# One hybrid mixer layer on Trainium2: high halves of split weights moved to ScalarE, SBUF-port exclusion put into the scheduler's model, two roots and their scans placed earlier, and the first step's low halves on VectorE

## The chip, the cores and the metric

The kernel runs on one core of one Trainium2 chip. The metric is the time on the device in microseconds (us), the median of three runs. The instruction engines are TensorE (PE in the profile, with its weight loads as PEld), VectorE (DVE; V in the code), ScalarE (ACT; A), GpSimd (POOL; G) and the DMA queues, which are issued from SyncE (SP).

## What is computed

A decoder trunk of two layers runs over T = 272 tokens (16 learned meta tokens ahead of 256) of D = 1024 channels. Layer 0's mixer is one projection whose columns feed two heads side by side (SSD and RG-LRU), then one output projection; layer 1's mixer is a multiscale causal pooling. Each layer ends in a hierarchical mixture of experts (MoE). Only layer 0's mixer is touched here:

```python
def ssd_lru_mixer(hn, w_in, ..., w_out):
    proj = hn @ w_in
    z, xbc, dt_raw, lru_gate, lru_in = jnp.split(proj, [i1, i2, i3, i4], axis=-1)
    y_ssd = ssd_mixer(z, xbc, dt_raw, ...)
    xb = causal_depthwise_conv(lru_in, lru_conv_w, lru_conv_b)
    y_lru = rg_lru(xb, lru_w_a, ...) * jax.nn.gelu(lru_gate, approximate=True)
    return jnp.concatenate([y_ssd, y_lru], axis=-1) @ w_out
# end of ssd_mixer: one root mean square for each of 2 groups of 512 channels
    y = y.reshape(bsz, l, SSD_WIDTH) * jax.nn.silu(z)
    yg = yg * lax.rsqrt(jnp.mean(yg * yg, axis=-1, keepdims=True) + RMS_EPS)
# in rg_lru: a root for each channel and token, then a scan along the tokens
    mult = jnp.sqrt(-jnp.expm1(2.0 * log_a))
    u = mult * (i * xf)          # h[t] = a[t] * h[t-1] + u[t]
```

## The kernel before, in words

The engines' program is recorded first and ordered afterwards. A class `Program` wraps the engines; each call is recorded as an `Op` with an estimated duration, and `order()` places the recorded ops on the engines by a list scheduler that works on those estimates. It also fills gaps of TensorE with small dummy products (`wm`, L735 at the start). So every instruction shows the recorder's line, L102, in the profile, and tiles rather than lines tell them apart. A change of an estimate, or of where a piece of work is recorded, changes the order of the instructions on every engine.

`mixer0()` runs in 26 steps of 256 weight columns. Steps 0 to 17 multiply the normed tokens by `w_in`, steps 18 to 21 multiply the SSD output `ys` by the upper half of `w_out`, steps 22 to 25 the LRU output `yl` by the lower half. The products are made in a reduced format at nearly full precision: each operand is split into a high half and a low half, and three products are added (Xh·wh, Xl·wh, Xh·wl). With 8 slices of 128 input channels (`k`), 2 blocks of 128 columns and 3 products, a step has 48 matmuls into two PSUM tiles `pj`.

The f32 weight tile `w` of a step is split in three parts by the plan `SPLIT_IN`/`SPLIT_OUT`: slices 0 to 3 (tiles of 128x1024) and 4 and 5 (128x512) get their high half `wh` from ScalarE and their low half `wl` = w − wh from VectorE; slices 6 and 7 get both halves from GpSimd. A pool of 7 buffers holds them, so that a step's halves can only be made when a buffer of about two steps earlier has been read. `split_act` makes the halves of `ys` and `yl`: ScalarE the high one, GpSimd the low one. In step 0, whose parts are split finer, slices 0 to 3 have other makers: VectorE makes some high halves, GpSimd the low ones.

Between the projections stands the heads' own work, placed by `at(step, function)`: the conv, gates and quads of the SSD (`mq`, `yp`, `xT`), the gated and normed SSD output (`z_gate`, whose sums of squares over 512 channels go through TensorE products `gss`; `group_norm` with its root on ScalarE and its reciprocal `rg` on VectorE), the LRU's gates (`lru_gates`, tiles `lr`, `li`, `xb`), its root (`lru_sqrt`, one ScalarE instruction on 8 tiles `lq`) and its 8 scans (`lru_scan`), then `lru_out` with the gate. Before, `z_gate` stands at step 15, `lru_sqrt` and `group_norm` at 16, the scans at 17 and 18.

Weight tiles are loaded by SyncE in a fixed order into 17 slots; the table `HELD` sets how many slots the heads' tiles keep at each step. After the mixer comes the MoE, whose expert weights stream through the same slots.

## Time and profile before

| | |
|---|---|
| runs | 737.16 us median of 3 (736.65 to 738.29) |
| profiled execution | 736.74 us; its span 735.1 us |
| mean granted TensorE clock | 0.978 of full speed |
| PE / DVE / ACT / POOL busy | 696.8 / 314.8 / 245.2 / 148.8 us |
| bytes moved | 234 MB, 318 GB/s over the span |

The mixer of layer 0 takes the first 215 us or so of the span. The busy times are sums over the whole span; a row of the timeline has the start in us from the span's start, the busy time in us, the engine, the line, the operation, the tiles (output, then inputs), the shapes and the number of equal instructions in a row; in square brackets stand the idle time of the engine just before it and what ended that.

### The profile page before, as it was taken

Reading aid. Unit: us, or ns where it says so; the run is one execution under the profiler, and the core shown is the slowest. Engines: PE = TensorE matmul, PEld = TensorE weight load, DVE = VectorE, ACT = ScalarE, POOL = GpSimd, SP = SyncE. Lnnn points to the kernel's source line nnn. Section 1 sums busy time; section 2 is a strip of 40 time slices with the busy share of each in tenths; the row PEclk is TensorE's granted clock in tenths of the full one; section 3 lists DMA queues with packets and bytes.
Section 4 is the critical chain, followed back from the end, with each engine's and each line's share of the span. In section 5 each row is a group of like instructions: output and inputs, shape, how many; then the busy total and the mean of one; then the engine's idle time right before and its main releaser. Section 6 shows DMA issues by size and latency. Waiting matters only on the chain. (4 is left out here: it accounts for less than half of the span.)

```text
span 735.1 us, 10978 instructions
## 1 busy us (share of the span) xinstructions
PE 696.8 (95%) x4309; PEld 442.7 (60%) x4309; DVE 314.8 (43%) x701; ACT 245.2 (33%) x466; POOL 148.8 (20%) x149
## 2 busy tenths in 40 slices
PE   6999999997999999999996999999999999989995
PEld 5989898997899556346343544585444453443344
DVE  6879799769965312022022014544120220302114
ACT  5565485785353232112110301452212121121114
POOL 5554685557751000000000012000000000000003
PEclk7999999999999999999998999999999999999998
DMA  8994021945574879999999999998799999999995
GB/s 258 242 349 151 20 63 62 326 135 214 207 284 170 290 293 411 409 409 409 409 409 408 409 399 377 400 408 306 296 405 409 408 409 409 409 408 408 409 385 155
DMA packets 99622, 234.06 MB, mean 318 GB/s; under 512 B 12700, under 2 KB 51800, under 8 KB 99560
## 3 DMA queue, kind: packets, MB, share of 16 engines
q1 hardware_dynamic: 97448, 232.72, 84.0%
q8 instruction: 37, 0.61, 0.3%
q10 hardware_dynamic: 2112, 0.52, 0.3%
q14 instruction: 25, 0.20, 0.1%
HBM read 232.18 MB, written 1.05 MB: 317 GB/s over the span
## 5 line engine op out<-in xcount | busy, mean ns | idle before, releaser
L102 PE MATMUL yb<-w,ht 128*64 128x512 f32 (+2 forms) x592 | 114.9, 538 | 2.3 <-ACT ht L102 2.0
L102 PE MATMUL gb<-w,xg 128*64 128x512 f32 x496 | 114.0, 597 | 0.0
L102 PE MATMUL ub<-w,xg 128*64 128x512 f32 (+1 forms) x514 | 112.9, 581 | 0.0
L102 PE MATMUL pj<-Xh,wh 128*128 128x272 f32 x288 | 85.8, 300 | 1.3 <-DVE xT L102 1.3
L102 PE MATMUL pj<-Xl,wh 128*128 128x272 f32 x288 | 84.4, 294 | 0.0
L102 PE MATMUL pj<-Xh,wl 128*128 128x272 f32 x288 | 84.1, 293 | 0.0
L102 PEld LDWEIGHTS ub<-w,xg 128*64 128x64 f32 x514 | 37.4, 137 | 70.5 <-issue 68.8
L102 PEld LDWEIGHTS yb<-w,ht 128*64 128x64 f32 x592 | 40.6, 137 | 64.4 <-issue 53.7
L102 DVE SCALAR_TENSOR_TENSOR yl<-yb,gs,yh 128x512 fp32r<-128x512 f32 (+2 forms) x37 | 25.1, 677 | 124.6 <-ACT yh L102 115.4
L102 DVE SCALAR_TENSOR_TENSOR sg<-ub,gs,sg 128x512 f32<-128x512 f32 x16 | 12.0, 751 | 153.4 <-PE ub L102 152.0
L102 PEld LDWEIGHTS gb<-w,xg 128*64 128x64 f32 x496 | 33.6, 136 | 61.1 <-issue 57.5
L102 DVE TENSOR_TENSOR wl<-w,wh 128x1024 fp32r<-128x1024 f32 (+1 forms) x50 | 59.5, 1200 | 16.8 <-PE pj L102 9.1
L102 ACT ACTIVATE xg<-xgp,gain_e 128x256 f32<-128x256 f32 x64 | 30.2, 475 | 97.2 <-PE xgp L102 78.7
L102 POOL TENSOR_TENSOR fo<-hT,gfin 128x256 f32<-128x256 f32 (+1 forms) x10 | 6.1, 630 | 277.7 <-DVE hT L102 277.5
L102 POOL TENSOR_SCALAR wh<-w 128x512 fp32r<-128x512 f32 x25 | 52.1, 2084 | 31.9 <-PE pj L102 23.9
L102 DVE TENSOR_TENSOR hT<-cmb,hT 128x272 f32<-128x272 f32 (+3 forms) x102 | 44.9, 495 | 29.7 <-PE cmb L102 29.6
L102 PEld LDWEIGHTS pj<-Xh,wh 128*128 128x128 f32 x288 | 55.4, 194 | 2.7 <-DVE xT L102 1.5
L102 ACT ACTIVATE yh<-yb,gs 128x512 fp32r<-128x512 f32 (+2 forms) x37 | 23.3, 630 | 98.2 <-PE yb L102 98.2
L102 PEld LDWEIGHTS pj<-Xl,wh 128*128 128x128 f32 x288 | 55.4, 193 | 0.2
L102 PEld LDWEIGHTS pj<-Xh,wl 128*128 128x128 f32 x288 | 55.3, 193 | 0.0
L102 ACT CAST wh<-w 128x512 fp32r<-128x512 f32 (+1 forms) x51 | 42.0, 829 | 31.8 <-PE pj L102 18.8
L102 POOL TENSOR_TENSOR wl<-w,wh 128x512 fp32r<-128x512 f32 x29 | 41.8, 1445 | 40.6 <-issue 19.1
(348 smaller groups left out, 1022.4 us busy)
## 6 DMA issues: line engine op xcount, KB each, us to landing
w<-in_expert_w_down_dram SPq DMA_DIRECT2D x63, 1024.0 KB, 17.2
w<-in_expert_w_gate_dram SPq DMA_DIRECT2D x62, 1024.0 KB, 18.0
w<-in_expert_w_up_dram SPq DMA_DIRECT2D x62, 1024.0 KB, 15.6
w<-in_w_in_dram SPq DMA_DIRECT2D x17, 1024.0 KB, 9.1
w<-in_w_out_dram SPq DMA_DIRECT2D x8, 1024.0 KB, 11.7
ew<-in_expert_w_gate_dram SPq DMA_DIRECT2D x4, 512.0 KB
xs<-in_x_dram SPq DMA_DIRECT2D x2, 512.0 KB
w<-in_w_in_dram SPq DMA_DIRECT2D x2, 512.0 KB
```

Of the source, the lines that this page charges most:

```text
L102: return prog.add(key, lambda: call(*a, **k), reads, writes, prog.cost(key, method, out, reads, k), func)
```

## The change

Six edits are made, all in the mixer of layer 0 and in the scheduler that orders it:

1. In `SPLIT_IN` and `SPLIT_OUT` the high half of slices 6 and 7 goes from GpSimd to ScalarE. The low half stays on GpSimd.
2. `order()` gets a resource `port`: a VectorE op with two wide SBUF inputs (or a VectorE copy or tensor_scalar from SBUF to SBUF) and a GpSimd tensor_tensor or tensor_scalar never overlap in the model. This alters the order only, nothing is enforced on the chip.
3. In step 0 all high halves go to ScalarE and the low halves of slices 0 to 3 to VectorE, after the normed tokens.
4. `split_act` makes the low halves of `ys` and `yl` on VectorE.
5. The two roots of the group norm get a function of their own, `group_root`, at step 13, after `z_gate` (moved from 15 to 13); `lru_sqrt` is cut into tiles 0 to 5 at step 13 and 6 and 7 at step 15; scans 0 to 5 stand at steps 15 to 17; `group_norm` goes from 16 to 15.
6. `HELD` of steps 14, 15 and 16 goes from 9, 8, 10 to 11, 10, 8.

```diff
+    def port(self, key, method, out, reads):
+        wide = [r for r in reads if self.cols(r) > 1 and not self.in_psum(r)]
+        if key == "G":
+            return method in ("tensor_tensor", "tensor_scalar")
+        return key == "V" and (len(wide) > 1 or (method in ("tensor_scalar", "tensor_copy") and len(wide) == 1
+                                                 and not self.in_psum(out)))
...
                     s = max(c, op.est, s)
+                    if op.port:
+                        s = max(s, port)
...
+                if op.port:
+                    port = op.end
...
-        SPLIT_IN = [(0, 4, A, V), (4, 2, A, V), (6, 2, G, G)]
-        SPLIT_OUT = [(0, 4, A, V), (4, 2, A, V), (6, 2, G, G)]
+        SPLIT_IN = [(0, 4, A, V), (4, 2, A, V), (6, 2, A, G)]
+        SPLIT_OUT = [(0, 4, A, V), (4, 2, A, V), (6, 2, A, G)]
...
-        split_part(0, parts, 0, 2, None, G)
...
         normed(0, 1, V)
+        split_part(0, parts, 0, 2, None, V)
...
-                    split_part(0, parts, k, 2, V, None)
-                    split_part(0, parts, k, 2, None, G)
+                    split_part(0, parts, k, 2, A, None)
+                    split_part(0, parts, k, 2, None, V)
...
             A.copy(hi[:, k, :], val)
-            G.tensor_tensor(lo[:, k, :], val, ff(hi[:, k, :]), op=ALU.subtract)
+            V.tensor_tensor(lo[:, k, :], val, ff(hi[:, k, :]), op=ALU.subtract)
+
+        def group_root():
+            st["rg"] = [b1("rg") for _ in range(2)]
+            for g in range(2):
+                A.activation(st["rg"][g], st["gs"][g][:, :T], AF.Sqrt, scale=1.0 / 512.0, bias=eps_t)
...
+        at(13, z_gate)
+        at(13, group_root)
+        at(13, lru_sqrt, 0, 6)
+        at(14, alloc_hl, "ys")
...
-        at(15, z_gate)
-        at(16, lru_sqrt)
-        at(16, alloc_hl, "ys")
-        at(16, group_norm)
-        at(16, hs_free, 2)
-        for t in range(4):
-            at(17, lru_scan, t)
-        for t in range(4, 8):
+        for t in range(6):
+            at(15 + t // 2, lru_scan, t)
+        at(15, lru_sqrt, 6, 8)
+        at(15, group_norm)
+        at(15, hs_free, 2)
+        for t in range(6, 8):
             at(18, lru_scan, t)
...
-    HELD = [4, 4, 4, 4, 4, 4, 7, 7, 9, 10, 11, 13, 12, 8, 9, 8, 10, 8, 6, 6, 6, 4, 4, 4, 4, 4]
+    HELD = [4, 4, 4, 4, 4, 4, 7, 7, 9, 10, 11, 13, 12, 8, 11, 10, 8, 8, 6, 6, 6, 4, 4, 4, 4, 4]
```

The order on the engines moves with it. From step 18 on, TensorE's instructions stand nearly as before, apart from some that are drawn a little ahead, and in the MoE and in layer 1 exactly as before; SyncE issues the same loads in the same order. Two places on VectorE are shown.

The first is VectorE before the first products of step 0: the short chain of 3-column ops that ends in the norm's factor `rs_107`, and the first normed tokens `xn_94`. Before, it reads:

```order
L102 TENSOR_SCALAR xh0_109<-ss_106 128x3
L102 RECIPROCAL rs_107<-sq0_108 128x3
L102 TENSOR_SCALAR wh_118<-w_97 128x512
L102 TENSOR_TENSOR sq0_108<-rs_107 128x3
L102 TENSOR_TENSOR sq0_108<-sq0_108,xh0_109 128x3
L102 SCALAR_TENSOR_TENSOR rs_107<-sq0_108,rs_107 128x3
L102 TENSOR_SCALAR xn_94<-xs_91,rs_107 128x512
```

Now:

```order
L102 TENSOR_SCALAR xh0_109<-ss_106 128x3
L102 RECIPROCAL rs_107<-sq0_108 128x3
L102 TENSOR_TENSOR sq0_108<-rs_107 128x3
L102 TENSOR_TENSOR sq0_108<-sq0_108,xh0_109 128x3
L102 TENSOR_TENSOR wl_119<-w_97,wh_118 128x512
L102 SCALAR_TENSOR_TENSOR rs_107<-sq0_108,rs_107 128x3
L102 TENSOR_SCALAR xn_94<-xs_91,rs_107 128x512
```

A high half (`wh_118`) has left VectorE, a low half (`wl_119`) has come into the chain, and GpSimd has no low half to make there any more. On TensorE five more dummy products `wm` stand ahead of the transposes of `xn`.

The second is VectorE ahead of the last `w_in` step, step 17, whose low halves for slices 0 to 3 are `wl_349` before and `wl_355` now (step 16's are `wl_341` and `wl_346`). Before, from step 16's first low half on:

```order
L102 TENSOR_TENSOR wl_341<-w_291,wh_340 128x1024
L102 SCALAR_TENSOR_TENSOR xb_263<-thi_333,xb_263 128x272
L102 SCALAR_TENSOR_TENSOR xb_263<-thi_336,xb_263 128x272
L102 TENSOR_TENSOR wl_343<-w_291,wh_342 128x512
L102 TENSOR_TENSOR wl_349<-w_292,wh_348 128x1024
L102 SCALAR_TENSOR_TENSOR lq_276<-la_275,lq_276 128x272 x2
L102 TENSOR_TENSOR lq_276<-lq_276,xb_263 128x272 x2
L102 RECIPROCAL rg_354<-rg_354 128x272
L102 TENSOR_TENSOR wl_351<-w_292,wh_350 128x512
L102 SCALAR_TENSOR_TENSOR xT_145<-xT_145,prm_a_80,rg_354 128x272 x4
L102 RECIPROCAL rg_355<-rg_355 128x272
L102 TENSOR_TENSOR wl_362<-w_307,wh_361 128x1024
```

Now, the same stretch is longer; its first part

```order
L102 TENSOR_TENSOR wl_346<-w_291,wh_345 128x1024
L102 RECIPROCAL rg_324<-rg_324 128x272
L102 SCALAR_TENSOR_TENSOR lq_276<-la_275,lq_276 128x272 x2
L102 TENSOR_TENSOR lq_276<-lq_276,xb_263 128x272 x2
L102 TENSOR_SCALAR lq_276<-xb_263 128x1 x2
L102 SCALAR_TENSOR_TENSOR xb_263<-la_275,lq_276 128x272
L102 TENSOR_TENSOR wl_348<-w_291,wh_347 128x512
L102 SCALAR_TENSOR_TENSOR xb_263<-thi_337,xb_263 128x272
L102 SCALAR_TENSOR_TENSOR xb_263<-la_275,lq_276 128x272
L102 SCALAR_TENSOR_TENSOR xT_145<-xT_145,prm_a_80,rg_324 128x272 x3
```

and the rest up to step 17's low half

```order
L102 SCALAR_TENSOR_TENSOR xb_263<-thi_340,xb_263 128x272
L102 SCALAR_TENSOR_TENSOR xT_145<-xT_145,prm_a_80,rg_324 128x272
L102 TENSOR_TENSOR ys_334<-xT_145,ys_333 128x272
L102 RECIPROCAL rg_325<-rg_325 128x272
L102 TENSOR_TENSOR ys_334<-xT_145,ys_333 128x272 x3
L102 SCALAR_TENSOR_TENSOR xT_145<-xT_145,prm_a_80,rg_325 128x272 x3
L102 TENSOR_TENSOR ys_334<-xT_145,ys_333 128x272
L102 SCALAR_TENSOR_TENSOR xT_145<-xT_145,prm_a_80,rg_325 128x272
L102 TENSOR_TENSOR wl_355<-w_292,wh_354 128x1024
```

Before, step 17's low half came right behind step 16's, and step 18's (`wl_362` before) had the norm's two reciprocals `rg` and the gated outputs `xT` ahead of it; now those, the low halves of `ys` and two of the scans stand ahead of step 17's. TensorE has four products of step 17, four of step 18 and one dummy in front of the first that needs `wl_355`, and the sums of squares `gss` stand ahead of step 14, where before they stood behind step 15.

## Rows read from the trace of the kernel before

**Rows 1.** Page, part 1: busy time, share of the span and instructions of each engine.
```profile
PE 696.8 (95%) x4309; PEld 442.7 (60%) x4309; DVE 314.8 (43%) x701; ACT 245.2 (33%) x466; POOL 148.8 (20%) x149
```

**Rows 2.** Windows (PE, PEld, DVE, ACT, POOL busy; PEclk, DMA share, GB/s), MoE.
```profile
270.00:280.00 10.00, 10.00 (x50) 3.37 (x48) 1.50 (x2) 2.06 (x3) 0.00 (x0) 1.00 1.03 410
```

**Rows 3.** Timeline of PE: first transposes, and five waits over half a us.
```profile
12.39 0.69 PE L102 MATMUL xn<-ident,xn 128*128 128x128 f32 x2 [3.80 <-ACT mne L102]
...
111.64 0.39 PE L102 MATMUL pj<-Xh,wh 128*128 128x272 f32 x1 [1.28 <-DVE xT L102]
...
174.21 0.39 PE L102 MATMUL pj<-ys,wl 128*128 128x272 f32 x1 [0.78 <-POOL wl L102]
...
179.90 0.39 PE L102 MATMUL pj<-ys,wl 128*128 128x272 f32 x1 [3.92 <-DVE wl L102]
...
189.18 0.52 PE L102 MATMUL pj<-ys,wl 128*128 128x272 f32 x2 [0.95 <-DVE wl L102]
...
201.51 0.40 PE L102 MATMUL pj<-yl,wl 128*128 128x272 f32 x1 [0.57 <-DVE wl L102]
```

**Rows 4.** Windows, columns as in the second group, behind three of these waits.
```profile
12.39:19.70 7.31, 7.31 (x28) 5.46 (x29) 5.67 (x12) 3.73 (x8) 3.47 (x3) 0.50 0.88 263
111.64:115.30 3.66, 3.66 (x17) 3.66 (x18) 3.66 (x11) 2.15 (x4) 1.50 (x2) 0.55 0.55 175
179.90:183.60 3.70, 3.70 (x17) 3.70 (x18) 3.70 (x11) 0.00 (x0) 0.00 (x0) 0.55 1.02 411
```

**Rows 5.** Timeline of DVE, start of the program.
```profile
8.91 0.15 DVE L102 TENSOR_TENSOR sq<-rs 128x3 f32<-128x3 f32 x1
9.10 1.26 DVE L102 TENSOR_TENSOR sq<-sq,xh 128x3 f32<-128x3 f32 x1
10.39 1.18 DVE L102 SCALAR_TENSOR_TENSOR rs<-sq,rs 128x3 f32<-128x3 f32 x1
```

**Rows 6.** Timeline of POOL, at the same place.
```profile
9.08 2.48 POOL L102 TENSOR_TENSOR wl<-w,wh 128x512 fp32r<-128x512 f32 x2 [1.76 <-DVE sq L102]
```

**Rows 7.** Timeline of DVE, step 11, ahead of TensorE's wait at 111.64.
```profile
108.40 2.78 DVE L102 TENSOR_TENSOR mq<-mq,cbm 128x512 f32<-128x512 f32 x2
```

**Rows 8.** Timeline of POOL, same place, and a low half and outputs later.
```profile
109.59 1.92 POOL L102 TENSOR_SCALAR wh<-w 128x512 fp32r<-128x512 f32 x1
...
159.83 1.29 POOL L102 TENSOR_TENSOR wl<-w,wh 128x512 fp32r<-128x512 f32 x1 [1.42 <-issue]
...
196.81 3.57 POOL L102 TENSOR_TENSOR yl<-xb,yl 128x272 fp32r<-128x272 f32 x4
```

**Rows 9.** Timeline of PE: the products that begin behind steps 14 and 15.
```profile
147.77 0.62 PE L102 MATMUL lr<-xb,lw 128*128 128x272 f32 x2
...
155.61 1.08 PE L102 MATMUL gss<-z,ones 128*128 128x272 f32 x4
```

**Rows 10.** Timeline of DVE, steps 14 to 23.
```profile
147.90 1.23 DVE L102 TENSOR_TENSOR wl<-w,wh 128x1024 fp32r<-128x1024 f32 x1 [1.10 <-issue]
...
152.81 0.69 DVE L102 TENSOR_TENSOR wl<-w,wh 128x512 fp32r<-128x512 f32 x1 [0.93 <-PE pj L102]
...
158.81 1.84 DVE L102 RECIPROCAL rg<-rg 128x272 f32<-128x272 f32 x1
...
180.37 0.78 DVE L102 SCALAR_TENSOR_TENSOR lq<-la,lq 128x272 f32<-128x272 f32 x2
181.07 0.78 DVE L102 TENSOR_TENSOR lq<-lq,xb 128x272 f32<-128x272 f32 x2
...
181.96 1.33 DVE L102 TENSOR_TENSOR_SCAN xb<-la,lq 128x272 f32<-128x272 f32 x2
...
194.69 4.32 DVE L102 TENSOR_TENSOR xb<-xb,gt 128x272 f32<-128x272 f32 x4
```

**Rows 11.** Timeline of ACT: the table load ahead of the LRU's root.
```profile
153.75 1.28 ACT L102 ACT_TABLE_LOAD   x1
```

**Rows 12.** Groups of instructions by line and shape, 20 to 235 us.
```profile
L102 ACT CAST wh<-w 128x512 fp32r<-128x512 f32 x25 | 15.5, 621 | 10.6 <-DVE hT L102 10.2 <-issue 0.3
```

## The prediction

> **What bounds the kernel.** The page's first part comes first: TensorE is busy 95% of the span, VectorE, ScalarE and GpSimd 43, 33 and 20% [rows 1]. Time can come from TensorE's idle time, from its clock, or from nowhere. The timeline of TensorE, filtered for waits, shows where it idles in the mixer: 3.80 us before the first transposes, 1.28 in step 11, then 0.78, 3.92, 0.95 and 0.57 in the w_out steps [rows 3]. [...] Last, a window in the MoE shows where the mixer's time goes: TensorE is busy without a gap while the DMA runs at 410 GB/s, share 1.03 [rows 2]. The MoE's instructions keep their order, so I let what is saved in the mixer arrive at the end one to one. The weight stream could swallow some of it, since its loads start when slots come free; but the slots come free by the mixer's own products, so they move with it.

> **The start.** VectorE's chain to the norm's factor holds two 3-column ops of 1.26 and 1.18 us, where such an op just before took 0.15 [rows 5]. Beside both lies a GpSimd subtraction from 9.08 to 11.56 [rows 6]. The change takes that subtraction off GpSimd. The two ops then cost some 0.3 together instead of 2.44; a 128x512 low half that now stands between them costs 0.69 [rows 10]; the high half that left the chain is worth little. So the transposes start 2.44 − 0.3 − 0.69 = 1.4 us earlier; I count 1.3. The second part is the clock. The idle time before the transposes (3.80) falls by the same 1.3, and five dummy products stand in what is left. The 7.31 us from 12.39 on ran at 0.50 [rows 4]; at full clock the same work would need 3.7. It is not all TensorE's to win, as the tokens' normed halves come from VectorE and ScalarE meanwhile: VectorE is busy 5.67 of the 7.31. Bounds: 1.1 (the clock stays low, and GpSimd's absence gives only the shorter chain) and 4.2 (the clock comes back before the transposes, 1.3 plus 80% of 3.7). I take 2.5, between them, since the dummies fill part of the gap only.

> **Step 11.** The wait of 1.28 ends on an `xT` that stands behind a pair of `mq` products of 2.78 us [rows 3, 7]; the same kind of op with two SBUF inputs takes, by the nearest clean row, 0.78 for two of 272 columns [rows 10], so two of 512 columns should take some 1.4. A GpSimd cast of 1.92 us lies beside the second of them [rows 8]; it goes to ScalarE. Afterwards 3.66 us at 0.55 lose 3.66 × 0.45 = 1.65 [rows 4], so 2.9 hang on this place. In the new order that `xT` still stands behind the pair and also behind a 128x512 low half. Bounds: +2.9 (wait and drop both go) and −1 (the wait grows by the low half's 0.69 and a little). I take 0.9: the wait falls by some 0.7, the drop shortens a little. Smaller waits in the early steps I leave out.

> **The w_out steps.** Before, they cost 0.78 + 3.92 + 0.95 + 0.57 = 6.2 of waits [rows 3] and 3.70 × 0.45 = 1.7 by the clock [rows 4]: 7.9. All wait for a low half: GpSimd's or VectorE's. The change sends two streams the other way: 25 casts and 16 subtractions leave GpSimd, the 16 come to VectorE at half of 0.78, 0.39 each [rows 10], 6.2 in all. To price what is left I add up VectorE's new chain from the end of step 14, where a buffer comes free for `wl_346`, to step 17's `wl_355`. It holds two 1024-wide low halves (1.23 each), two reciprocals (1.84 each), four `lq` products (0.39 each), two scans (1.33 for both), one 512-wide low half (0.69) [rows 10], and 15 ops of 272 columns (2 `xb`, 8 `xT`, 5 `ys`) at 0.39 to 0.4: 2.46 + 3.68 + 1.56 + 1.33 + 0.69 + 5.9 = 15.6; with half a us for hand-overs (each `ys` low half waits for ScalarE's high one) some 16. TensorE needs `wl_355` after the LRU gates and step 15, 155.61 − 147.77 = 7.84, step 16 (the same without the gates, two `lr` at 0.62 and two `li` like them: 6.6) [rows 9], and eight products of 48 and a dummy, 1.1: 15.5. `gss` does not delay it any more, as it stands ahead of step 14. So a wait of 0.5 is left; in the stretch lie also two GpSimd low halves of 1.29 [rows 8], each of which may hold VectorE up for its length: 0 to 3.1 in all. I take 1.5, with 0.3 more for step 18's low half (VectorE and TensorE have some 6 of work each behind `wl_355`), and 0.7 for `gss`, which in its new place waits for `z` (0 to 1.3). The clock may drop once more at a shorter wait; I put 0.1. Later steps lose nothing: VectorE's four `xb` of 4.32 us, beside which GpSimd's `yl` ran [rows 8, 10], become some 1.6, and this pays for the 8 `yl` low halves of 0.39. Gain: 7.9 − 1.5 − 0.3 − 0.7 − 0.1 = 5.3; bounds 1.8 (3.1 of wait at step 17 with a drop of 1.7, and 1.3 for `gss`) and 7.9.

> [...]

> **What I cost at nothing.** ScalarE gets 25 casts of 0.62, 15.5 us [rows 12], and one table load more, 1.28 [rows 11], since the root is made in two goes. It is busy a third of the span [rows 1] and the high halves may be made a step ahead of their use; if that cover went, a late `wh` would cost up to 0.62 a step. The new `HELD` leaves SyncE's order, so loads only shift; nothing waits for a `w` in the stretch.

> **Sum.** 2.5 + 0.9 + 5.3 = 8.7 against the profiled execution of 736.74, which lies 0.42 under the median of the runs. So 728.0 for such an execution, and 728.5 against the median.

> **Rivals.**
> - *The waits go, and the clock with them.* If the dummies keep the clock up at the start (4.2), step 11 stays clean (2.9) and the w_out steps lose hardly anything (7.5), the gain is 14.6: 722.5. For it: every drop follows an idle stretch. Against: VectorE's chain before step 17 has no slack by the sum above.
> - *Half of it.* The start keeps its low clock (1.1), step 11 nothing, and step 17 waits 3.1 with a drop behind it and 0.3 at step 18, so the late gain is 2.8: 3.9 in all, 733.3. For it: step 17's chain is long and in one piece.
> - *VectorE becomes the bound in steps 17 to 21 (slower).* It gets the 16 `ys` and `yl` low halves while GpSimd keeps one low half a step, 1.29, against which VectorE's two-input ops stop. The wait per step must exceed 7.9/5 = 1.6 us over these five steps to eat the late gain; with a start and a middle worth 1.1 and 0, it decides from 1.8 on. At 2.4 a step: 12 − 7.9 − 1.1 = 3 slower, 740. For it: four products worth 1.6 took 4.32 beside GpSimd [rows 8, 10]. Against: that was four GpSimd ops in a row, and one is left.
> - *Waits only move (no change).* Step 17's wait takes the place of step 18's 3.92 with its clock drop, step 11 gets 1 worse, and the start gives 1.1: within 1.5 us of 737.

> **Chances and range.** 0.2% of this time, 1.5 us, is about what a measurement of this kernel can tell from no change. The forecast with its own 724 to 732 gets 0.54, the larger gain 0.11, the half 0.19, no change 0.07, slower 0.09. Faster: 0.54 + 0.11 + 0.19 = 0.84; same 0.07; slower 0.09. The range takes in the half, most of the larger gain and the bounds of the late wait: 721.5 to 736.

> **What would show it.** In the changed profile: the 3-column ops near 9 us take 0.15 to 0.2 each, and the first transposes start near 11; the clock over the next 7 us is above 0.50. `mq` takes near 1.4 for two in step 11. The wait of 3.92 at step 18 is gone, and the largest one in the w_out steps is for step 17's low half, 1 to 2 us, with VectorE busy all through the stretch before it. No wait of TensorE's ends on ScalarE's `wh`. I am wrong in the mechanism if the largest wait still stands at step 18, if `wh` is waited for, or if time is won or lost behind 270 us, where nothing was reordered.

## The result, and the profile after

The changed kernel takes 729.19 us (median of 4 runs, 728.79 to 731.21) against 737.72 for the kernel before (4 runs): ratio 0.9891, 95% interval 0.9867 to 0.9914. The forecast was 728.5. The profiled execution took 729.16 us with a span of 727.1 (736.74 and 735.1 before).

The page's first part answers to [rows 1]; GpSimd's busy time fell from 148.8 to 83.0 and ScalarE's rose by 15.5:

```profile
PE 693.5 (95%) x4315; PEld 439.1 (60%) x4315; DVE 304.8 (42%) x718; ACT 260.7 (36%) x496; POOL 83.0 (11%) x104
```

The timeline of TensorE, its first transposes and the waits from step 11 to step 20, answers to [rows 3]:

```profile
11.05 0.44 PE L102 MATMUL xn<-ident,xn 128*128 128x128 f32 x2 [1.73 <-ACT xn L102]
...
108.72 0.39 PE L102 MATMUL pj<-Xh,wh 128*128 128x272 f32 x1 [0.85 <-DVE xT L102]
...
159.09 0.78 PE L102 MATMUL pj<-ys,wh 128*128 128x272 f32 x4 [0.36 <-ACT wh L102]
161.45 0.52 PE L102 MATMUL pj<-Xh,wl 128*128 128x272 f32 x2 [1.47 <-DVE wl L102]
174.09 0.52 PE L102 MATMUL pj<-ys,wl 128*128 128x272 f32 x2 [0.85 <-DVE wl L102]
180.40 0.40 PE L102 MATMUL pj<-ys,wl 128*128 128x272 f32 x1 [0.30 <-DVE wl L102]
```

The wait of 3.92 at step 18 is gone; the largest one, 1.47, is at the first product that needs step 17's low half. A wait on a high half of ScalarE's has come in, 0.36.

To see where time went I take the start of four pieces of work on TensorE as landmarks; they stand in the same order in both kernels: the first transposes `xn`, the first `dtt` products (behind step 4), the `yp` products on either side of step 11, and the ranks `rk` of the MoE's router, just behind the mixer.

| | xn | dtt | yp | yp | rk | end of span |
|---|---|---|---|---|---|---|
| before | 12.39 | 52.44 | 106.09 | 119.00 | 240.81 | 735.1 |
| changed | 11.05 | 50.95 | 103.59 | 114.54 | 230.89 | 727.1 |
| won so far | 1.34 | 1.49 | 2.50 | 4.46 | 9.92 | 8.0 |

So in these two executions the start gave 1.5, steps 5 to 10 gave 1.0, step 11 gave 2.0, the rest of the mixer 5.5, and the MoE and layer 1, in which nothing was changed, took 1.9 back.

The start on VectorE (it answers to [rows 5]): the 3-column ops take 0.16, with a low half between them.

```profile
9.04 0.16 DVE L102 TENSOR_TENSOR sq<-rs 128x3 f32<-128x3 f32 x1
9.24 0.16 DVE L102 TENSOR_TENSOR sq<-sq,xh 128x3 f32<-128x3 f32 x1
9.34 0.69 DVE L102 TENSOR_TENSOR wl<-w,wh 128x512 fp32r<-128x512 f32 x1
9.95 0.15 DVE L102 SCALAR_TENSOR_TENSOR rs<-sq,rs 128x3 f32<-128x3 f32 x1
```

Step 11 on VectorE and on GpSimd (they answer to [rows 7] and [rows 8]): no cast lies beside `mq` any more, but GpSimd's own `mq` products do until 107.1, and the pair still takes 2.37, where 1.4 was forecast.

```profile
105.89 2.37 DVE L102 TENSOR_TENSOR mq<-mq,cbm 128x512 f32<-128x512 f32 x2
108.19 0.89 DVE L102 SCALAR_TENSOR_TENSOR xT<-xT,dsk,yp 128x272 f32<-128x272 f32 x2
```

```profile
103.61 3.50 POOL L102 TENSOR_TENSOR mq<-mq,BC 128x512 f32<-128x512 f32 x2 [0.48 <-ACT mq L102]
```

VectorE's chain ahead of step 17, from `wl_346` to `wl_355` (it answers to [rows 10]); between the lines shown it has no idle time:

```profile
144.36 1.23 DVE L102 TENSOR_TENSOR wl<-w,wh 128x1024 fp32r<-128x1024 f32 x1 [2.17 <-PE pj L102]
145.50 1.85 DVE L102 RECIPROCAL rg<-rg 128x272 f32<-128x272 f32 x1
...
149.43 1.72 DVE L102 TENSOR_TENSOR wl<-w,wh 128x512 fp32r<-128x512 f32 x1
...
158.74 1.51 DVE L102 SCALAR_TENSOR_TENSOR xT<-xT,prm_a,rg 128x272 f32<-128x272 f32 x1
160.18 1.21 DVE L102 TENSOR_TENSOR wl<-w,wh 128x1024 fp32r<-128x1024 f32 x1
```

It ends at 161.39, 17.0 after its start; the sum gave 16. Two ops are longer than they are alone, 1.72 for 0.69 and 1.51 for 0.4, and beside each lies a low half of GpSimd's:

```profile
149.24 1.36 POOL L102 TENSOR_TENSOR wl<-w,wh 128x512 fp32r<-128x512 f32 x1 [5.90 <-PE pj L102]
158.33 1.63 POOL L102 TENSOR_TENSOR wl<-w,wh 128x512 fp32r<-128x512 f32 x1 [7.72 <-PE pj L102]
```

### The profile page after: what moved, and what is told of

Read it like the earlier page. It is cut to its first block, busy times and chain, and to the rows that moved or that the text cites. A ratio compares the mean times of both kernels' runs of the same rounds, so it can differ in the third digit from the quotient of the medians.

```text
span 727.1 us, 10969 instructions
## 1 busy us (share of the span) xinstructions
PE 693.5 (95%) x4315; PEld 439.1 (60%) x4315; DVE 304.8 (42%) x718; ACT 260.7 (36%) x496; POOL 83.0 (11%) x104
## 5 line engine op out<-in xcount | busy, mean ns | idle before, releaser
L102 ACT CAST wh<-w 128x512 fp32r<-128x512 f32 (+1 forms) x79 | 57.0, 757 | 23.3 <-PE pj L102 17.9
L102 DVE TENSOR_TENSOR wl<-w,wh 128x512 fp32r<-128x512 f32 (+1 forms) x54 | 53.6, 998 | 19.3 <-PE pj L102 8.3
L102 ACT ACTIVATE sg<-gb,gs 128x512 f32<-128x512 f32 x16 | 11.0, 687 | 93.1 <-PE gb L102 93.1
L102 PE MATMUL xgp<-S,hnt 128*128 128x256 f32 x256 | 38.8, 295 | 2.3 <-PEq L1598 2.3
```

Of the source, the lines that this page charges most:

```text
L102: op = prog.add(key, lambda: call(*a, **k), reads, writes, prog.cost(key, method, out, reads, k), func)
```

## The experiments

The profiled executions of all kernels, with the same pieces of work. The differences of the last columns are the ones to compare, since the first 20 us also vary from execution to execution: the last eight transposes of `raw` take 1.09 in most profiles and 1.97 in that of e3_old_roots. How much is seen in e3 and e5, whose engines run the change's own order up to 137 and 154 us: they reach `dtt` at 50.85 and 52.45, the change at 50.95. A single profile gives the differences, too, only to within a clock drop or two of some 1.6 us each, as e4 and e11_np show below.

| kernel | median us | ratio to before, interval | dtt | rk | dtt to rk | rk to end |
|---|---|---|---|---|---|---|
| before | 737.5 | | 52.44 | 240.81 | 188.4 | 494.3 |
| changed | 729.19 | 0.9891 [0.9867, 0.9914] | 50.95 | 230.89 | 179.9 | 496.2 |
| e1_hi_scalar | 739.28 | 1.0027 [1.0015, 1.0039] | 51.93 | 241.06 | 189.1 | 495.7 |
| e2_no_port | 729.54 | 0.9893 [0.9854, 0.9932] | 50.30 | 232.35 | 182.1 | 496.4 |
| e3_old_roots | 729.86 | 0.9895 [0.9866, 0.9924] | 50.85 | 238.66 | 187.8 | 488.9 |
| e4_old_start | 732.52 | 0.9936 [0.9907, 0.9964] | 52.71 | 234.19 | 181.5 | 496.2 |
| e5_lo_gpsimd | 732.69 | 0.9933 [0.9908, 0.9959] | 52.45 | 237.42 | 185.0 | 494.1 |
| e7_first_step | 732.95 | 0.9939 [0.9921, 0.9958] | 48.45 | 236.53 | 188.1 | 494.4 |
| e8_shift70 | 728.86 | 0.9888 [0.9864, 0.9912] | 49.68 | 229.71 | 180.0 | 495.1 |
| e10_hi_gpsimd | 729.98 | 0.9893 [0.9866, 0.9919] | 51.36 | 241.97 | 190.6 | 488.9 |
| e9_shift30 | 723.59 | 0.9810 [0.9778, 0.9842] | 50.95 | 230.91 | 180.0 | 488.9 |
| e11_np | 729.59 | 0.9881 [0.9846, 0.9917] | 49.29 | 230.73 | 181.4 | 498.8 |
| e11_30 | 722.47 | 0.9787 [0.9750, 0.9825] | 50.12 | 229.99 | 179.9 | 490.7 |
| e12_before_shift | 730.77 | 0.9906 [0.9874, 0.9938] | 52.61 | 240.96 | 188.4 | 487.8 |

### Edit 1 alone

```diff
-        SPLIT_IN = [(0, 4, A, V), (4, 2, A, V), (6, 2, G, G)]
+        SPLIT_IN = [(0, 4, A, V), (4, 2, A, V), (6, 2, A, G)]
```

and the same for `SPLIT_OUT`, on the kernel before.

> The kernel before with the first edit alone: the high halves of slices 6 and 7 go from GpSimd to ScalarE, nothing else is touched. My theory (the gain is a sum of parts with different causes): the start stays as before (first transposes at 12.4), the wait of step 11 and the small waits of the early steps shrink (2 to 3 us together), and the w_out steps keep about half of their 7.9, since the group norm's reciprocals still stand ahead of step 18's low half; in all 4 to 5 us faster than before, 732 to 734. Rival, one edit does it all (the casts on GpSimd were what held VectorE up): 729 to 730, as the whole change. Second rival, the casts were hidden: 736 to 738.

Measured 739.28, slower by 0.15 to 0.39%. My theory and both rivals missed; the second came nearest. Relieving GpSimd of 52 us of casts gained nothing in sum: from `dtt` to `rk` it took 189.1 us against 188.4. Between the two landmarks of step 11 it won 1.9 (10.98 for 12.91): the wait fell from 1.28 to 0.88, and the clock stayed full. Ahead of them it lost 1.5 (55.11 from `dtt` to `yp`, 53.65 before), with a wait of 0.69 ahead of `acs` (0.32 before) and a low clock further on:

```profile
73.82 0.59 PE L102 MATMUL acs<-adt,mle 128*128 128x16 f32 x4 [0.69 <-ACT wh L102]
```

```profile
89.50:93.20 3.70, 3.70 (x20) 3.70 (x19) 3.70 (x10) 2.13 (x4) 2.70 (x2) 0.59 0.09 21
```

The first row names a cast of ScalarE's, which ended at 73.71; what `acs` reads is VectorE's `adt`, done at 73.68. Behind step 11 it lost the other 1.2. VectorE's timeline in the stretch before step 18:

```profile
160.74 3.55 DVE L102 RECIPROCAL rg<-rg 128x272 f32<-128x272 f32 x2
164.22 5.63 DVE L102 SCALAR_TENSOR_TENSOR xT<-xT,prm_a,rg 128x272 f32<-128x272 f32 x8
169.78 2.95 DVE L102 TENSOR_TENSOR wl<-w,wh 128x1024 fp32r<-128x1024 f32 x2
```

The scheduler now puts the two reciprocals and all eight `xT` ahead of the low halves, and the `xT` beside GpSimd's `ys` low halves take 0.70 each, where they took 0.56 and 0.65 before and 0.43 with nothing beside them. TensorE waits 2.89 at 171.61, and its granted clock over the next 3.7 us is 0.57; further waits of 1.44 (`wl`) and 2.29 (`hT`) follow.

### The port in the model

```diff
-                    op.port = prog.port(key, method, out, reads)
+                    op.port = False
```

> The whole change, but the scheduler orders the instructions without the port exclusion. My theory: with the casts gone from GpSimd few collisions are left, so the model changes the order at a few places only and the time by at most 1.5 us, 729 to 731. Rival, the model is what makes the new order good: waits of several us come back in steps 16 to 19, 733 or more.

Measured 729.54, by the medians as the change: my theory held for the time. In the profile it loses 2.1 us from `dtt` to `rk` (182.1 for 179.9), and its start is 0.65 earlier at `dtt`. All of the loss lies ahead of step 11 (55.10 from `dtt` to `yp`, 52.64 in the change), where TensorE waits 0.68 ahead of `acs` at 72.16 and runs at 0.57 from 88.30 to 92.00; the change has neither. The waits in steps 16 to 19 that the rival named did not come: 0.36 and 1.48 stand there, as in the change.

### The old places of the roots and scans

```diff
-        at(13, z_gate)
-        at(13, group_root)
-        at(13, lru_sqrt, 0, 6)
-        at(14, alloc_hl, "ys")
...
+        at(15, z_gate)
+        at(16, lru_sqrt, 0, 8)
+        at(16, alloc_hl, "ys")
+        at(16, group_root)
...
-    HELD = [4, 4, 4, 4, 4, 4, 7, 7, 9, 10, 11, 13, 12, 8, 11, 10, 8, 8, 6, 6, 6, 4, 4, 4, 4, 4]
+    HELD = [4, 4, 4, 4, 4, 4, 7, 7, 9, 10, 11, 13, 12, 8, 9, 8, 10, 8, 6, 6, 6, 4, 4, 4, 4, 4]
```

with `group_norm` and the scans back at 16 to 18, on the changed kernel.

> The whole change with the old places of the roots, the group norm, z_gate and the scans, and the old HELD (edits 5 and 6 undone). My theory: the gain of 5.5 us in the w_out steps rests about half on these places; the reciprocals come again between step 17's and step 18's low halves, TensorE waits 2 to 3.5 us at step 18 and its clock may drop behind it: 731.5 to 734. The start and step 11 stay as in the change (transposes at 11.1). Rival, the places do nothing once GpSimd is relieved: 729 to 730. Second rival, the old places are better, since VectorE's chain before step 17 gets shorter: below 728.

The time, 729.86, was that of the first rival, and the profile contradicts it: the mixer ends 7.8 us later than in the change. The scheduler put dummies ahead of these waits, so that part of the idle time looks busy. TensorE's timeline, dummies and waits of steps 18 to 20:

```profile
164.99 2.34 PE L751 MATMUL wm<-ident 128*128 128x128 f32 x20
...
168.19 0.52 PE L102 MATMUL pj<-ys,wl 128*128 128x272 f32 x2 [0.86 <-DVE wl L102]
...
174.32 3.44 PE L751 MATMUL wm<-ident 128*128 128x128 f32 x30
...
187.16 0.52 PE L102 MATMUL pj<-ys,wl 128*128 128x272 f32 x2 [2.10 <-DVE wl L102]
```

So the places are worth 187.8 − 179.9 = 7.9 us in the mixer, over twice what I expected, and the loss was made good behind it: `rk` to the end took 488.9 instead of 496.2. Where, two rows say. TensorE's first product behind the overflow branch of the first MoE (a test whether more tokens chose an expert than fit; its body is jumped over) in the kernel before

```profile
401.98 0.55 PE L102 MATMUL xgp<-S,hn 128*128 128x256 f32 x1 [5.95 <-PEq L1576]
```

and in the change

```profile
392.19 0.55 PE L102 MATMUL xgp<-S,hn 128*128 128x256 f32 x1 [6.08 <-PEq L1598]
```

wait 5.95 and 6.08 us for TensorE's own sequencer (`PEq`); with the old places it is 1.68. This became a question of its own, below.

### The old first step

```diff
         split_part(0, parts, 0, 2, A, None)
+        split_part(0, parts, 0, 2, None, G)
...
-        split_part(0, parts, 0, 2, None, V)
...
-                    split_part(0, parts, k, 2, A, None)
-                    split_part(0, parts, k, 2, None, V)
+                    split_part(0, parts, k, 2, V, None)
+                    split_part(0, parts, k, 2, None, G)
```

> The whole change with the first step's halves as before (edit 3 undone: some high halves on VectorE, the low ones on GpSimd). My theory: GpSimd's low half again lies beside the 3-column ops, which take over 1 us each, and the transposes start at 12.3 to 12.5; 1.3 to 1.6 us slower than the change, 730.5 to 731. Rival, in the change ScalarE bounds the rest of step 0, so what is lost ahead of the transposes is won behind them: 728.5 to 729.5.

Measured 732.52, 3.3 us over the change, twice the expected amount; the rival is out. Not all of it is the start's: the profile is 1.8 behind the change at `dtt` and 3.3 at `rk`. The 1.5 between come with a clock drop behind the wait for step 17's low half, 1.48 here and 1.47 in the change, which kept its clock:

```profile
163.22:166.92 3.70, 3.70 (x17) 3.70 (x18) 3.70 (x11) 3.67 (x5) 0.00 (x0) 0.54 0.39 126
```

and in the change

```profile
161.45:165.15 3.70, 3.70 (x29) 3.70 (x30) 3.70 (x11) 3.67 (x5) 0.00 (x0) 1.00 0.44 125
```

At the start the expected mechanism is there. On GpSimd four low halves now run from 8.59 to 14.05, and on VectorE the whole chain lies beside them:

```profile
8.70 1.20 DVE L102 TENSOR_TENSOR sq<-rs 128x3 f32<-128x3 f32 x1
...
10.15 1.22 DVE L102 TENSOR_TENSOR sq<-sq,xh 128x3 f32<-128x3 f32 x1
...
11.63 1.21 DVE L102 SCALAR_TENSOR_TENSOR rs<-sq,rs 128x3 f32<-128x3 f32 x1
12.88 1.46 DVE L102 TENSOR_SCALAR xn<-xs,rs 128x512 f32<-128x512 f32 x1
```

Three ops of 0.16 take 1.2 each, and the transposes start at 13.65, later than in the kernel before.

### The low halves of ys and yl on GpSimd

```diff
-            V.tensor_tensor(lo[:, k, :], val, ff(hi[:, k, :]), op=ALU.subtract)
+            G.tensor_tensor(lo[:, k, :], val, ff(hi[:, k, :]), op=ALU.subtract)
```

> The whole change, but the low halves of ys and yl stay on GpSimd (edit 4 undone). My theory (two-input ops of VectorE and GpSimd's subtractions stop each other): 16 subtractions come back beside VectorE's reciprocals, xT and xb products of steps 15 to 23; these show mean times 1.5 to 2 times as long again, the largest waits of the w_out steps grow to 3 us or more, and the mixer's end (the router's first product, 230.9 in the change) comes 2 to 4 us later. Rival, VectorE is the crowded engine in that stretch and would be relieved by it: the mixer's end comes at 230 or earlier.

The mixer's end came at 237.42, and `dtt` to `rk` took 5.1 more than in the change; the time is 3.5 over it. TensorE's two largest waits grow to

```profile
162.08 0.39 PE L102 MATMUL pj<-Xh,wl 128*128 128x272 f32 x1 [1.94 <-DVE wl L102]
...
170.02 0.39 PE L102 MATMUL pj<-ys,wl 128*128 128x272 f32 x1 [2.67 <-DVE wl L102]
```

and the clock over the 3.7 us behind the second is 0.60. The mechanism of my expectation missed in part: the 272-column products of VectorE are not 1.5 to 2 times as long over the whole mixer (`xT` 0.63 on average for 0.62, `xb` 0.57 for 0.57). Others are, just where TensorE waits: step 17's two low halves take 2.96 beside GpSimd's `ys` (1.21 and 0.68 in the change).

```profile
160.25 2.96 DVE L102 TENSOR_TENSOR wl<-w,wh 128x1024 fp32r<-128x1024 f32 x2
```

```profile
159.10 4.75 POOL L102 TENSOR_TENSOR ys<-xT,ys 128x272 fp32r<-128x272 f32 x4 [0.83 <-ACT ys L102]
```

The four `lq` products behind them take 4.35, against 1.56 in the change.

### Edit 3 alone

```diff
-        split_part(0, parts, 0, 2, None, G)
...
+        split_part(0, parts, 0, 2, None, V)
...
-                    split_part(0, parts, k, 2, V, None)
-                    split_part(0, parts, k, 2, None, G)
+                    split_part(0, parts, k, 2, A, None)
+                    split_part(0, parts, k, 2, None, V)
```

on the kernel before.

> The kernel before with edit 3 alone, the first step's halves of the change. My theory: the 3-column ops take 0.2 each again, the transposes start near 11.1, and steps 0 and 1 end 1.3 to 1.5 earlier than before; nothing else moves, 735.5 to 736.5. Rival (the casts on ScalarE hold step 0 up as much as GpSimd did): 737 to 738.

Measured 732.95: 4.4 us faster, three times the expected amount. Transposes at 10.15, and the granted clock is back by 16 us, against about 20 before. Windows of 2 us (columns as in [rows 2]):

```profile
12.00:14.00 2.00, 2.00 (x10) 1.98 (x10) 2.00 (x6) 1.80 (x4) 0.55 (x1) 0.52 0.38 49
14.00:16.00 2.00, 2.00 (x11) 1.64 (x11) 0.61 (x2) 0.74 (x2) 0.95 (x1) 0.62 0.94 289
16.00:18.00 2.00, 2.00 (x16) 1.75 (x15) 1.76 (x3) 1.66 (x5) 0.00 (x0) 1.00 1.10 367
```

From `dtt` to `rk` it is as before (188.1 for 188.4), so all of it is won in the first steps.

### Edit 1 taken out of the whole change

```diff
-        SPLIT_IN = [(0, 4, A, V), (4, 2, A, V), (6, 2, A, G)]
+        SPLIT_IN = [(0, 4, A, V), (4, 2, A, V), (6, 2, G, G)]
```

and the same for `SPLIT_OUT`, on the changed kernel.

> The whole change, but the high halves of slices 6 and 7 stay on GpSimd (edit 1 undone). My theory now: edit 1 alone gave nothing, since VectorE's order was made without knowing of the collisions and the reciprocals stood badly; but with the rest in place GpSimd's casts of 2 us collide again with VectorE's chain, so the mixer's end comes 4 us or more later than in the change (235 or later). Rival (edit 1 is idle in the whole change too): mixer's end at 230 to 232. The time at the end may come out lower than that says, as this program has 48 more products ahead of the overflow branch.

The mixer's end came at 241.97, 11.1 us later than in the change and later than before the change: edit 1, worth nothing alone, is worth 10.7 us from `dtt` to `rk` when the rest is there. GpSimd's group of casts from 20 to 240 us:

```profile
L102 POOL TENSOR_SCALAR wh<-w 128x512 fp32r<-128x512 f32 x24 | 45.3, 1888 | 31.2 <-PE pj L102 30.1 <-PE pt L102 1.1
```

The expected collisions explain little of it: VectorE's `mq` and `xT` are shorter than in the change (0.86 and 0.49 on average for 1.26 and 0.62), its `ys` and `yl` longer (0.60 and 0.58 for 0.42 and 0.43), some 2.6 us over all 16. TensorE stands before step 17's low half with 39 dummies and a wait, where the change has one dummy and 1.47:

```profile
161.19 4.42 PE L751 MATMUL wm<-ident 128*128 128x128 f32 x39
...
166.96 0.52 PE L102 MATMUL pj<-Xh,wl 128*128 128x272 f32 x2 [1.35 <-DVE wl L102]
```

What makes VectorE late there is not traced to its end. The time at the end, 729.98, hides the loss as in e3: behind the branch TensorE waits 1.64 only.

### The wait of the sequencer

The two kernels without the wait had more products ahead of the branch. The edit puts tiny products of 16 columns, 70 at first, on TensorE at the very start, in place of some dummies; the lines that define the tiny product are not shown:

```diff
...
+                if not self.shifted:
+                    self.shifted = True
+                    for _ in range(70):
+                        out.append(self.tiny)
+                    gap -= 70 * 40
...
```

> The change, with 70 tiny products (16 columns) on TensorE at the very start, in place of the 12 dummies there, while it waits for the first load. Theory (from the run with the old places, which had 56 more products ahead of the overflow branch in the first MoE and showed no 6 us wait of TensorE's sequencer there): that wait comes from where the branch lies in TensorE's instruction stream, and 58 more instructions take it away in this kernel too, and the one of 2.3 us in the second MoE: 721 to 725. Rival (the wait is absent there since TensorE reached the branch later, when what it waits for was ready): the wait stays 6 us and the time 728.5 to 730.

Missed: the wait is 6.04, the time 728.86. But a tiny product is two matmul records of the profile (4443 in all, 4315 in the change), and the profile has as many weight loads as matmuls (4315 of each in the change): 128 records more are 256 instructions more. The two kernels without the wait have 56 and 49 records more, 112 and 98 instructions; those with it lie between −12 and +32. With the wait back at +256, the place may repeat, after 256 instructions or a part of that; this was a guess from these places. The next kernel has 30 in place of 70 in the same edit.

> The change with 30 tiny products at the very start for 5 of the dummies there. Theory (the 6 us wait at the overflow branch depends on the branch's place in TensorE's stream modulo 256 instructions): counted in matmul records of the profile, weight load and product each, the kernels with the wait lie at −12 to +32 from the change, the two without it at +98 and +112, and the one with 70 tiny products, which kept the wait, at +256, which is the same place again. This one lies at +110: the wait at the first branch falls from 6.1 to 1.6 to 1.7, at the second from 2.3 to 1.1, and the clock dip behind the first goes: 721 to 724.5. Rival (the wait goes only where TensorE comes late to the branch, as it did in those two): 6 us stay, 727 to 730.

723.59, ratio 0.9810 [0.9778, 0.9842]. TensorE's first product behind the branch, and windows of 2 us behind it, in this kernel:

```profile
387.80 0.35 PE L102 MATMUL xgp<-S,hn 128*128 128x256 f32 x1 [1.64 <-DVEq L1605]
```

```profile
387.80:389.80 2.00, 2.00 (x17) 2.00 (x18) 1.77 (x9) 0.95 (x2) 0.00 (x0) 1.00 1.04 410
```

The mixer is the change's to a few hundredths (`dtt` 50.95, `rk` 230.91 for 230.89), and TensorE came to the branch as early as there (the wait begins at 387.80 − 1.64 = 386.16, in the change at 392.19 − 6.08 = 386.11), so a late arrival is not what takes the wait away. The same 30 on the kernel before:

> The kernel before with the 30 tiny products alone (+98 in the same count). By the place of the branch: the waits of 5.95 and 2.48 fall to 1.7 and 1.1, and the kernel before gains 5.5 to 8 us without any of the change, 729.5 to 732. By the rival (a late arrival is what takes the wait away): 736.5 to 738.

730.77: the kernel before gains 6.6 us by 30 tiny products and nothing of the change; its waits fall to 1.64 and 1.07. So in these kernels the wait goes with the place of the branch in TensorE's stream: 6.08 became 1.64 at +110 (e9), 5.95 became 1.64 at +98 (e12), and at +256 it was 6.04 (e8). The runs do not fix a period, as 128 would fit the same places as well as 256, and no trace shows what the sequencer does in these 6 us.

### Step 0 without the port in the model

```diff
-                    op.port = prog.port(key, method, out, reads)
+                    op.port = prog.ported and prog.port(key, method, out, reads)
...
+        prog.ported = False
...
+        prog.ported = True
```

`ported` is false from the start of the mixer to the end of step 0.

> The change with the port exclusion left out of the model for step 0 alone. Theory (in the change the exclusion puts a second cast and two copies on ScalarE ahead of the ops that the transposes wait for, 0.9 us against the kernel before with edit 3 alone): transposes near 10.2 instead of 11.05, and 1 to 2 us off the time, 727 to 728.5. Rival (the start is set by the state of the clock, not by this order): 728.5 to 730.

The transposes start at 10.15 as expected, and `dtt` comes 1.66 earlier; yet the time is 729.59. Of its four executions the profiled one is the slowest, 731.52, and two took 728.1 and 728.6. In the profile 1.5 is lost at step 11, by the same wait as in the change but with another clock behind it, and 2.6 more than in the change behind `rk` (498.8). TensorE's wait, and the window behind it (0.64; in the change 1.00):

```profile
106.97 0.39 PE L104 MATMUL pj<-Xh,wh 128*128 128x272 f32 x1 [0.88 <-DVE xT L104]
```

```profile
106.97:110.65 3.68, 3.68 (x20) 3.68 (x21) 3.68 (x13) 2.15 (x4) 1.46 (x2) 0.64 0.57 200
```

The same with the 30 tiny products:

> Both together: 30 tiny products at the start (+100 in the count of the run with 30 alone) and no port exclusion in step 0. If both theories hold, 719.5 to 723; if only the place of the branch counts, 722 to 724; if neither, 728 to 730.

722.47, ratio 0.9787 [0.9750, 0.9825]: the fastest of all, and faster than both kernels. Against e9 (0.9810) the intervals overlap, so whether the start's share of it is real stays open.

## Why the prediction was right, point by point

**The start (forecast 2.5, measured 1.5).** The mechanism was right: the 3-column ops fell from 1.26 and 1.18 to 0.16 [rows 5], and the transposes came 1.34 earlier (1.3 forecast). The clock was the part sized wrong. The dummies did not hold it up: over 11.05 to 18.36 it was 0.58, against 0.50 before [rows 4]. What the term is worth depends on the order around it and on the execution: 4.4 us alone (e7), over my upper bound of 4.2, and 1.8 at `dtt` when taken out of the change (e4). e3 and e5, with the change's start, reach `dtt` 1.6 and 0.0 ahead of the kernel before, so the 1.5 is one draw among such. In the change ScalarE has more to do ahead of the transposes than in e7, and these start 0.9 later.

**Steps 5 to 10 (left out, measured 1.0).** TensorE's idle time there fell from 0.58 to nothing; the other 0.4 is not traced.

**Step 11 (forecast 0.9, measured 2.0).** The wait fell by 0.43 (1.28 to 0.85), not 0.7, since GpSimd's own `mq` products stand where the cast stood. But the drop behind it did not come:

```profile
108.72:112.40 3.68, 3.68 (x29) 3.68 (x30) 3.68 (x13) 2.19 (x5) 1.45 (x2) 1.00 0.60 202
```

Ten profiles have a wait of 0.85 to 0.89 at this place: nine run at 1.00 behind it, e11_np, with 0.88, at 0.64. The three with 1.28 or 1.29 (before, e7, e12) run at 0.55 or 0.56. So at the shorter length the drop came in one of ten executions. I had taken half a gain where these showed nearly all or nothing.

**The w_out steps (forecast 5.3, measured 5.5 with all that follows in the mixer).** The chain to `wl_355` was summed to 16 and took 17.0; its wait was put at 1.5 and was 1.47; that one comes at step 17 and not at 18, as forecast. That the clock stayed full behind it was luck: the same wait of 1.47 or 1.48 is followed by 1.00 in the change, e8, e9, e11_np and e11_30, but by 0.59 in e2 and 0.54 in e4, at a cost of some 3.7 × 0.46 = 1.7 by e4's row, where I had set aside 0.1. Step 18's wait of 0.3 did not come; step 19 and 20 wait 0.85 and 0.30 instead (174.09, 180.40). `gss` shows no wait where 0.7 was set aside. Both GpSimd low halves of the stretch did stand in the way (149.24 to 150.60 beside the `wl` of 1.72, 158.33 to 159.96 beside the `xT` of 1.51) and cost VectorE 1.0 and 1.1; the wait of 1.47 stayed well under its upper bound of 3.1, as the rest of the chain ran 1.1 shorter than my sum with its hand-overs.

**One to one to the end (the assumption that was off).** 9.9 us were won by `rk` and 8.0 are left at the end. 1.1 of the loss lies between 402 and 408 of the kernel before: TensorE is back at full clock 4 us after the branch's wait, and 6 us after it in the change. Windows of 2 us, before:

```profile
404.00:406.00 2.00, 2.00 (x13) 2.00 (x12) 0.00 (x0) 0.86 (x2) 0.00 (x0) 0.61 1.02 403
406.00:408.00 2.00, 2.00 (x19) 2.00 (x18) 0.00 (x0) 1.52 (x4) 0.00 (x0) 1.00 1.04 412
```

and in the change:

```profile
394.20:396.20 2.00, 2.00 (x12) 2.00 (x11) 0.00 (x0) 0.85 (x2) 0.00 (x0) 0.50 1.04 412
396.20:398.20 2.00, 2.00 (x12) 2.00 (x12) 0.00 (x0) 0.81 (x3) 0.00 (x0) 0.57 1.01 399
```

Another 0.57 is a wait for the weight stream near the end, which the kernel before does not have:

```profile
702.38 1.94 PE L102 MATMUL ub<-w,xg 128*64 128x512 f32 x8 [0.57 <-DMA w<-in_expert_w_up_dram]
```

Over the kernels with the 6 us wait, `rk` to the end is 494.1 to 498.8, without any order among them that follows the mixer's gain; so the carrying is one to one within some 2 us. The misses, +1.2 in the mixer and −1.9 behind it, cancelled in part, so that the forecast came this close by luck as well as by its terms. The prediction had named time won or lost behind 270 us as a sign that its mechanism is wrong; that sign came, and it counts against this assumption, not against the terms in the mixer.

**ScalarE at nothing.** Nearly so: one wait on `wh`, 0.36 at 159.09, which the prediction had also named as a sign against it. At that size it leaves the account as it was.

**The slower rival** (VectorE the bound in steps 17 to 21) has its mechanism in e1 and e5, where GpSimd keeps the `ys` low halves and the waits grow to 2.7 to 2.9 with a clock drop behind them; in the change one low half a step was too little for it. That edit 1 alone would be slower was in none of my cases: I had added parts that only work together. Alone it is worth −0.7 us from `dtt` to `rk`, within the rest 10.7; the places of the roots are worth 7.9 within the rest.

## What to carry to other kernels

Moving work off an engine can gain nothing in sum where the order behind it is not made anew (52 us of casts left GpSimd in e1, and `dtt` to `rk` took 189.1 us for 188.4): look which work stands ahead of what TensorE waits for, and price the whole chain, not the engine's load. Compare variants at a landmark at the end of the changed stage, not at the end of the program: a wait at a branch, 6.08 us in the change and 1.68 and 1.64 in e3 and e10, made these two look equal to the change, though their mixers were 8 and 11 us slower. And when a program has a runtime branch, shift the stream ahead of it by some instructions and time it; here that gave 5.6 and 6.6 us, against 8.5 by the whole change. Where two kernels differ by 1 or 2 us, look at several executions: a clock drop of that size came and went between profiles whose order was the same at that place.
